# A transformer trunk on one core: the products with mod_w move from VectorE to TensorE, in strips of 32 columns, into the first mixer

## The chip, the cores and the metric

The kernel runs on one core of a Trainium2 chip. A core has TensorE (PE: matrix products into the eight banks of PSUM), VectorE (DVE), ScalarE (ACT), GpSimd (POOL) and SyncE (SP, which here issues the DMAs). Each works through a queue of its own in order, and semaphores tie them together. The metric is the device time of one execution in microseconds.

## What is computed

Two post-norm layers on a sequence of 512 tokens of width 1024. Before each of the four sub-layers (mixer and feed-forward in each layer) the input is scaled and shifted, and behind it the output is multiplied by a gate; all three come from a vector c:

```python
c_act = jax.nn.silu(c)
for l in range(DEPTH):
    mod = (c_act @ mod_w[l] + mod_b[l])[:, None, :]          # mod_w: (2, 1024, 6144)
    sh_m, sc_m, g_m, sh_f, sc_f, g_f = jnp.split(mod, 6, axis=-1)
    h = x * (1 + sc_m) + sh_m
    y = even_mixer(h, ...) if l % 2 == 0 else odd_mixer(h, ...)
    x = layer_norm(DEEPNORM_ALPHA * x + (1 + g_m) * y, ln_mix_g[l], ln_mix_b[l])
    h = x * (1 + sc_f) + sh_f
    y = conv_ffn(h, ...)
    x = layer_norm(DEEPNORM_ALPHA * x + (1 + g_f) * y, ln_ffn_g[l], ln_ffn_b[l])
```

The first mixer joins eight heads of sparse attention (an indexer keeps the best keys of a query by rounds of top-8) with eight heads of latent attention. The second is stick-breaking attention. mod_w is 48 MB in fp32 and is read once.

## The kernel before

All large products are made from float32r parts: an operand is split into a high and a low part, and a product is three (`mm3`: high-high, high-low, low-high). Weights come from DRAM by 128 x 512 tiles `raw`, are split by a cast to the high part on ACT (or DVE) and a subtraction on DVE or POOL into `whl`, and PE multiplies. Tensors stand transposed, 128 features by 512 tokens a tile. A product of two plain fp32 operands (the ones with `ones` or `ident`) needs more passes over the array; the trace shows it as two instructions, or as one where it is a transpose.

The stages in order of time: first projections (8 tiles of features, 7 banks open at once, from line 669; until about 73 us), late projections, index scores and top-k (until 168), four pairs of latent heads and four of sparse heads (until 300), the output product and norm (until 380), the feed-forward of layer 0 (up-projection until 612, down-projection and norm until 760), stick-breaking attention (until 1010) and its output and norm, then the feed-forward of layer 1.

**The products with mod_w.** In `m0` stand the shift and scale columns of the first mixer, which nothing can start without. For every k (128 features) ACT scales two of the eight 128 x 256 row blocks by columns of `ca` = silu(c), POOL adds them, DVE runs six more through `scalar_tensor_tensor` into half of the tile `xres` (named acc at line 672), and PE sums its 128 rows by products with a column of ones into the bank `cs`. From that come A_col and B_col, the scaled input hk, and its parts in `h`.

The other parts of mod_w go through `mod_acc` (line 937): for 512 columns at a time eight tiles `mraw` (two buffers) are loaded, and DVE adds m * ca to the tile `acc` (one buffer), eight `scalar_tensor_tensor` of 128 x 512. For parts 2 and 4 of layer 0, `shared`, the scaling and the sum are separate operations that POOL may take (`nc.lazy`). `mod_cols(dst)` sums the rows of four 128-column pieces by products with ones into columns and makes A_col and B_col of sub-layer dst; `mod_gate(i)` spreads the sum over all partitions with a 128 x 128 tile of ones and adds 1, into the tile `gate`. They run where the code calls them: gate 0 and columns 1 during the first mixer (with a bias MOD_BIAS of 1560 places in the order), gate 1 and columns 2 as filler of the first feed-forward, columns 3 and gate 2 between the heads of stick-breaking attention, gate 3 in the second feed-forward.

**What sets the order.** The class `Plan` records all engine calls and then issues them by a list schedule: at every step the engine whose clock is earliest takes the operation with the smallest place in the recorded order (plus `nc.bias`) among those whose inputs are there. It uses a price for every operation (`price`, line 200), a delay between engines (HOP), a model of DMA (360 bytes per ns, start, end), of PE's clock (`pe_time`), and of the SBUF ports that DVE and POOL share (`port`, `port_free`: an operation that would have to wait for the ports for longer than `tol` is passed over). Operations of `nc.either` and `nc.lazy` go to the engine that would end them first. So the emitted queues are fixed, and they are in the order that these prices give. Tiles of a tag take its buffers in recorded order (BUFS).

```python
            lhs, rhs = kw["lhsT"], kw["rhs"]
            op.work = size(rhs) * (1.6667 if lhs.dtype == F32 else 0.4167)
            if lhs.dtype == BF16:
                return max(op.work + 2.5, 56.0)
            return max(op.work + 2.5, size(lhs) * (1.6667 if lhs.dtype == F32 else 0.835))
```

Of the kernel before, what the change touches and what calls it, by code (L numbers as in the profile page):

```python
# [28 lines left out]
ROUNDS = min(256, S // 4) // 8  # L29
ALPHA = 4.0 ** 0.25  # L30
# [24 lines left out]
# ns from the end of an instruction to the start of one that waits for it  # L55
# [14 lines left out]
# what each hold of the SBUF ports shared by VectorE and GpSimd waits for  # L70
# [8 lines left out]
class Plan:  # L79
    """Records engine calls in program order and issues them in the order of a list schedule.  # L80

    Dependences are those of the recorded order (by tile and region); a tag's tiles take
    their buffers in the recorded order, so the schedule cannot run out of buffers where
    the recorded order does not.
    """
# [26 lines left out]
    # -- recording --  # L112
# [86 lines left out]
    # -- costs --  # L199
    def price(self, op):  # L200
# [42 lines left out]
    def port(self, op, e=None):  # L243
        """how an op holds the pair of SBUF ports that VectorE and GpSimd share"""
# [15 lines left out]
    # -- scheduling --  # L260
    def schedule(self):
# [21 lines left out]
        def offer(i):  # L283
            """op i has all its inputs; it can run once its new tiles have buffers"""
# [32 lines left out]
        def port_free(i, e):  # L317
            """when the pair of SBUF ports that VectorE and GpSimd share is free for op i"""
# [15 lines left out]
        def worth(i, e):  # L334
            """whether engine e would finish op i before any other that may run it"""
# [20 lines left out]
        def pe_time(op):  # L356
            """the time of a TensorE instruction at the clock that its activity allows"""
# [12 lines left out]
        while done < len(ops):  # L370
# [41 lines left out]
            op.start = clock[e]  # L412
            k = self.port(op)
# [35 lines left out]
class _Either:  # L449
    """Operations that several engines may run, whichever comes to it first."""  # L450
# [14 lines left out]
    def scale(self, out, src, by):  # L465
        """out = src * by, a column"""
# [3 lines left out]
    def norm(self, x, mean, scale, bias):  # L470
        """x = (x - mean) * scale in place; bias = -mean * scale"""
# [17 lines left out]
class Parts:  # L489
    """tiles of equal width that are indexed as one of shape [P, 2, columns]"""  # L490
# [21 lines left out]
def tile_trunk(ctx: ExitStack, tc: tile.TileContext, t: dict):  # L512
# [7 lines left out]
        "raw": 4, "whl": 6, "t2": 8, "hl": 9, "row": 2, "gate": 1, "mraw": 2, "acc": 1,  # L520
# [42 lines left out]
    def split(out_hi, out_lo, src, eng=nc.either):  # L563
        """src (on SBUF) = out_hi + out_lo"""
# [3 lines left out]
    def split_ps(out_hi, out_lo, src):  # L568
        """the same with src on PSUM"""
# [3 lines left out]
    def split_heads(tiles, src):  # L573
        """rows 64 h of src (on PSUM) into rows 0 of tile h"""
# [7 lines left out]
    def load_w(src, cols, eng=nc.lazy, tag="whl"):  # L582
        """a weight tile's float32r parts; src(lo, hi) gives its columns lo..hi on DRAM"""
# [22 lines left out]
    ones = const("ones", [P, P])  # L606
    nc.vector.memset(ones[:], 1.0)
    scr = tl("t2", [P, S])
    nc.gpsimd.memset(scr[:, 0:P], -1.0)
    nc.gpsimd.memset(scr[:, P:2 * P], -1.0)  # L610
    nc.gpsimd.affine_select(scr[:, P:2 * P], scr[:, P:2 * P], [[-1, P]], ALU.is_ge, 0.0, base=0, channel_multiplier=1)
    # negated ones and lower triangle, then the parts of the sparse values
    negs = const("negs", [P, 15, 64], F32R)
# [389 lines left out]
    def chain(*gens):  # L1003
        for g in gens:
            yield from g
# [628 lines left out]
```

## Time and profile before

| | us |
|---|---|
| median of 3 runs (lowest, highest) | 1409.38 (1405.83, 1412.77) |
| span of the profiled execution | 1414.6 |
| PE, DVE, ACT, POOL busy in it | 1337.3, 1102.1, 727.8, 333.9 |

The profile is of one execution; its span is 5.2 us above the median of the runs. A matmul's busy time reaches to the modelled end of its pipeline, so neighbours overlap, and the pace of products is read from one start to the next. All operations are recorded through one helper, so every instruction has line L446, and it is known by its tiles: `sc`, `tr`, `mm` and `md` are banks of PSUM, `t` are tiles t2, and buffer numbers are left out.

### The profile page before, as it was taken

Reading aid. Unit: us, or ns where it says so; the run is one execution under the profiler, and the core shown is the slowest. Engines: PE = TensorE matmul, PEld = TensorE weight load, DVE = VectorE, ACT = ScalarE, POOL = GpSimd, SP = SyncE. Lnnn points to the kernel's source line nnn. Section 1 sums busy time; section 2 is a strip of 40 time slices with the busy share of each in tenths; the row PEclk is TensorE's granted clock in tenths of the full one; section 3 lists DMA queues with packets and bytes.
Section 4 is the critical chain, followed back from the end, with each engine's and each line's share of the span. In section 5 each row is a group of like instructions: output and inputs, shape, how many; then the busy total and the mean of one; then the engine's idle time right before and its main releaser. Section 6 shows DMA issues by size and latency. Waiting matters only on the chain.

```text
span 1414.6 us, 21212 instructions
## 1 busy us (share of the span) xinstructions
PE 1337.3 (95%) x7468; PEld 1131.9 (80%) x7468; DVE 1102.1 (78%) x2030; ACT 727.8 (51%) x1376; POOL 333.9 (24%) x311
## 2 busy tenths in 40 slices
PE   4888799999899999999999999999969999999997
PEld 3666577887788999888877888878858999998885
DVE  6997997789898888883485886777688889994347
ACT  4355566753544444443334886788344555564230
POOL 4575866623611111020040100100041000020000
PEclk9987888999999999999999999999989999999999
DMA  9422433254155444553412243321305323242331
GB/s 323 149 66 65 131 97 107 90 165 134 60 165 170 133 156 153 174 168 107 134 42 93 75 146 112 108 82 60 104 30 176 116 98 120 89 150 93 101 105 59
DMA packets 88458, 166.54 MB, mean 118 GB/s; under 512 B 11128, under 2 KB 13688, under 8 KB 88352
## 3 DMA queue, kind: packets, MB, share of 16 engines
q1 hardware_dynamic: 88064, 165.14, 37.2%
q8 instruction: 58, 0.95, 0.3%
q14 instruction: 48, 0.39, 0.1%
q10 hardware_dynamic: 288, 0.06, 0.0%
HBM read 158.80 MB, written 2.10 MB: 114 GB/s over the span
## 4 chain that ended last, share of the span: by engine, by line
PE 71%; DVE 14%; issue 4%; ACT 4%; DMA 4%; POOL 2%; SPq 0%; DVEq 0%; POOLq 0%; ACTq 0%
PE sc L446 38%; PE tr L446 16%; PE mm L446 13%; PE md L446 4%; DVE t L446 4%; DVE xres L446 2%; DVE row L446 2%; ACT t L446 2%; DMA raw<-in_wup_dram 1%; DVE h L446 1%; DVE acc L446 1%; ACT qk L446 1%; DMA mraw<-in_mod_w_dram 1%; DVE hl L446 1%; DVE st L446 1%
## 5 line engine op out<-in xcount | busy, mean ns | idle before, releaser
L446 PE MATMUL sc<-h,whl 128*128 128x512 f32 (+1 forms) x2076 | 422.8, 359 | 7.8 <-ACT h L446 4.7
L446 PEld LDWEIGHTS sc<-h,whl 128*128 128x128 f32 x2076 | 348.7, 194 | 63.5 <-ACT h L446 5.5
L446 ACT CAST whl<-raw 128x512 fp32r<-128x512 f32 (+1 forms) x352 | 213.4, 613 | 264.0 <-PE sc L446 154.6
L446 DVE TENSOR_TENSOR whl<-raw,whl 128x512 fp32r<-128x512 f32 x296 | 207.8, 709 | 109.4 <-ACT whl L446 107.9
L446 POOL TENSOR_TENSOR whl<-raw,whl 128x512 fp32r<-128x512 f32 (+1 forms) x77 | 105.5, 1379 | 476.3 <-ACT whl L446 325.9
L446 DVE SCALAR_TENSOR_TENSOR acc<-mraw,ca,acc 128x512 f32<-128x512 f32 x118 | 98.0, 831 | 14.0 <-DMA mraw<-in_mod_w_dram 13.1
L446 POOL TENSOR_TENSOR rs<-rs,nhalf 128x1 f32<-128x1 f32 (+1 forms) x19 | 14.3, 754 | 328.5 <-DVE rs L446 328.4
L446 PE MATMUL sc<-whl,t 128*128 128x512 f32 x252 | 67.4, 393 | 0.3 <-ACT t L446 0.3
L446 ACT ACTIVATE t<-t 128x512 f32<-128x512 f32 x84 | 52.7, 637 | 19.5 <-DVE t L446 19.1
L446 DVE TENSOR_TENSOR raw<-raw,raw 128x512 f32<-128x512 f32 x86 | 59.1, 688 | 4.3 <-DMA raw<-in_wup_dram 2.8
L446 PE MATMUL mm<-h,whl 128*128 128x512 f32 x204 | 60.2, 435 | 1.2 <-ACT y L446 1.2
L446 ACT ACTIVATE t<-t,rs 128x512 f32<-128x512 f32 x16 | 13.0, 815 | 90.9 <-DVE rs L446 90.8
L446 PEld LDWEIGHTS sc<-whl,t 128*128 128x128 f32 x252 | 47.1, 188 | 11.3 <-DVE t L446 0.7
L446 PEld LDWEIGHTS mm<-h,whl 128*128 128x128 f32 x204 | 42.1, 212 | 11.5 <-ACT y L446 1.7
L446 ACT CAST hl<-t 128x512 fp32r<-128x512 f32 (+1 forms) x74 | 44.7, 627 | 5.4 <-DVE t L446 4.9
L446 PE MATMUL mm<-hl,V 128*128 128x128 f32 (+5 forms) x342 | 45.7, 276 | 1.2 <-ACT hl L446 0.9
L446 PEld LDWEIGHTS mm<-hl,V 128*128 128x128 f32 (+1 forms) x342 | 39.0, 168 | 8.0 <-ACT hl L446 2.1
L446 PE MATMUL tr<-whl,t 128*128 128x512 f32 x168 | 43.2, 391 | 0.0
L446 PE MATMUL mm<-whl,t 128*128 128x512 f32 x168 | 43.0, 391 | 0.0
L446 DVE SCALAR_TENSOR_TENSOR xres<-y,ca,xres 128x256 f32<-128x256 f32 x48 | 36.6, 773 | 8.0 <-POOL xres L446 7.2
L446 PE MATMUL tr<-h,whl 128*128 128x256 f32 (+1 forms) x240 | 40.1, 315 | 2.5 <-POOL whl L446 1.6
L446 PE MATMUL sc<-y,h 96*128 96x128 f32 (+3 forms) x96 | 34.4, 470 | 7.6 <-ACT y L446 3.2
(388 smaller groups left out, 2976.6 us busy)
## 6 DMA issues: line engine op xcount, KB each, us to landing
raw<-in_wup_dram SPq DMA_DIRECT2D x176, 256.0 KB, 3.4
mraw<-in_mod_w_dram SPq DMA_DIRECT2D x160, 256.0 KB, 2.9
raw<-in_wdown_dram SPq DMA_DIRECT2D x88, 256.0 KB, 2.9
y<-in_m_dram SPq DMA_DIRECT2D x16, 512.0 KB, 7.2
raw<-in_w_out_dram SPq DMA_DIRECT2D x32, 256.0 KB, 2.6
raw<-in_wqk_dram SPq DMA_DIRECT2D x32, 256.0 KB, 3.0
row<-in_ln_dram SPq DMA_DIRECT2D x8, 512.0 KB, 4.0
raw<-in_wqkv_dram SPq DMA_DIRECT2D x16, 256.0 KB, 3.0
```

Source lines behind the costliest of these rows:

```text
L446: getattr(getattr(self.nc, op.eng), op.fn)(*op.args, **op.kw)
```

## The change

The products with mod_w are made by PE with silu(c) as the stationary operand: a block of `cab` of 128 rows and 32 columns, one of which holds the values and the others zeros (a second row of the strip can be reached by shifting the window by one column, so that the two layers' gates share a strip). The result fills 32 partitions of a bank. Four column ranges of mod_w go to the four strips of partitions 0, 32, 64 and 96 of one bank. For `m0` the rows r and r + 4 share a strip, so the products of a k are eight of 32 x 256; ACT copies the bank to SBUF and the sum over the 128 rows by ones stays.

For the rest, `mod_rows` loads 128 x 512 tiles `mraw` (now four buffers) and makes one product of 32 x 512 with each: 32 for every `mod_cols`, 64 for the four gates together. Columns are then reached by four transposes of the bank's copy, gate rows wait in the constant tile `gate_rows` and are spread by a product of 32 rows (`sel`) when their gate is due. All of it is recorded behind the first projections with a bias of 200 places; only the spreading of a gate stays at its old place. `mod_acc` is gone, and with it the tags `acc` and `gate`; the bank `md` no longer serves the late projection and the norms of the latent vectors, which go to `mm` and `tr`. The constants `negones` and `negtri` are made later.

The planner changes in three places: a product with 32 stationary columns is priced at a quarter of its time, float32r products at some ns more, and DVE and POOL start an operation in the plan only once the ports are free. All else that the diff holds is removed comments.

```diff
@@ price
             lhs, rhs = kw["lhsT"], kw["rhs"]
             op.work = size(rhs) * (1.6667 if lhs.dtype == F32 else 0.4167)
+            if size(lhs) == COLS:
+                op.work /= P // COLS
+                return op.work + 2.5
             if lhs.dtype == BF16:
                 return max(op.work + 2.5, 56.0)
-            return max(op.work + 2.5, size(lhs) * (1.6667 if lhs.dtype == F32 else 0.835))
+            if lhs.dtype == F32:
+                return max(op.work + 2.5, size(lhs) * 1.6667)
+            return max(op.work + (13.0 if size(lhs) > 64 else 7.0), size(lhs) * 0.859)
@@ schedule
             op.start = clock[e]
+            if e in ("vector", "gpsimd"):
+                op.start = clock[e] = max(clock[e], port_free(i, e))
@@ tile_trunk
-        "raw": 4, "whl": 6, "t2": 8, "hl": 9, "row": 2, "gate": 1, "mraw": 2, "acc": 1,
+        "raw": 4, "whl": 6, "t2": 8, "hl": 9, "row": 2, "mraw": 4,
...
-    ca = const("ca", [P, KD])
-    nc.scalar.activation(ca[:], cT[:], AF.Silu)
+    cab = const("cab", [P, KD, COLS + 1])
+    nc.vector.memset(cab[:], 0.0)
+    nc.scalar.activation(cab[:, :, 1], cT[:], AF.Silu)
+    ca = lambda r, row: cab[:, r, 1 - row:1 - row + COLS]
...
         nc.bias = -150.0
-        acc = xa[:, 1, :].rearrange("p (a b) -> p a b", a=2)
-        row = lambda r: m0[r // 4][:, r % 4, :]
-        for r in range(MV_SPLIT, 8):
-            nc.scalar.mul(row(r), row(r), ca[:, r:r + 1])
-            if r > MV_SPLIT:
-                nc.gpsimd.tensor_tensor(acc[:, 1, :], row(r), acc[:, 1, :] if r > MV_SPLIT + 1 else row(MV_SPLIT), ALU.add)
-        nc.vector.scalar_tensor_tensor(acc[:, 0, :], row(0), ca[:, 0:1], acc[:, 1, :], ALU.mult, ALU.add)
-        for r in range(1, MV_SPLIT):
-            nc.vector.scalar_tensor_tensor(acc[:, 0, :], row(r), ca[:, r:r + 1], acc[:, 0, :], ALU.mult, ALU.add)
+        for r in range(KD):
+            g = r % 4
+            nc.tensor.matmul(cs[COLS * g:COLS * g + COLS, 0:256], lhsT=ca(r, 0), rhs=m0[r // 4][:, g, :], start=r < 4, stop=r >= 4, skip_group_check=True)
+        rk = xa[:, 1, 0:256]
+        nc.scalar.copy(rk, cs[:, 0:256])
...
+    def mod_rows(groups):
+        o = bank("md")
+        for i, (l, parts) in enumerate(groups):
+            for r in range(KD):
+                for g in range(4):
+                    lo = parts[g // 2] * D + (g % 2) * S
+                    m = tl("mraw", [P, S])
+                    nc.sync.dma_start(m[:], t["mod_w"][l, r * P:(r + 1) * P, lo:lo + S])
+                    nc.tensor.matmul(o[COLS * g:COLS * g + COLS, :], lhsT=ca(r, i), rhs=m[:], start=i == r == 0, stop=i == len(groups) - 1 and r == KD - 1, skip_group_check=True)
+        return o
+    def mod_cols(dst):
...
+        got = mod_rows([(l, (3 * sub_i, 3 * sub_i + 1))])
+        rows = tl("mraw", [P, S])
+        nc.scalar.copy(rows[:], got[:])
+        o = bank("md")
+        for j in range(4):
+            nc.tensor.transpose(o[:, j * P:(j + 1) * P], rows[:, j * P:(j + 1) * P], ident[:])
...
+    def mod_gates():
...
+        nc.vector.tensor_tensor(gate_rows[:], mod_rows([(l, (2, 5)) for l in range(2)])[:], gate_rows[:], ALU.add)
+    def mod_gate(i):
...
+            nc.tensor.matmul(o[:], lhsT=sel[rr, i // 2:i // 2 + 1].broadcast_to((COLS, P)), rhs=gate_rows[rr, :], start=True, stop=True)
+            nc.scalar.activation(g[:], o[:], AF.Identity, bias=ones[:, 0:1])
+    MOD_BIAS = 200.0
+    nc.bias = MOD_BIAS
+    mod_cols(1)
+    mod_gates()
+    mod_cols(2)
+    mod_cols(3)
...
-    us = ffn_up(0, h, chain(mod_gate(1), mod_cols(2)))
+    us = ffn_up(0, h, mod_gate(1))
...
-    steps = chain(mod_cols(3), mod_gate(2))
+    steps = mod_gate(2)
```

Where the change moves instructions on PE: first the head of its queue, the first projections. Before (`md_99` is cs, summed by ones from `xres`; sc, tr are banks of the projections):

```order
L446 MATMUL md_99<-ones,xres_102 128x1 x2
L446 MATMUL sc_92<-h_91,whl_103 128x512
L446 MATMUL sc_93<-h_91,whl_103 128x512
L446 MATMUL sc_92<-h_91,whl_103 128x512 x2
L446 MATMUL sc_93<-h_91,whl_103 128x512 x2
L446 MATMUL tr_94<-h_91,whl_103 128x512
L446 MATMUL md_99<-ones,xres_110 128x1 x2
```

and now (`y` holds m0, `cab` the strip):

```order
L454 MATMUL md_100<-y_101,cab 32x256 x4
L454 MATMUL md_100<-y_102,cab 32x256 x4
L454 MATMUL md_100<-ones,xres_103 128x1 x2
L454 MATMUL md_100<-y_109,cab 32x256 x4
L454 MATMUL sc_93<-h_92,whl_104 128x512
L454 MATMUL md_100<-y_110,cab 32x256 x4
L454 MATMUL sc_93<-h_92,whl_104 128x512 x2
```

The m0 products of a k stand in two groups of four, between the products of the k before.

Then PE at the late projections (`mm` are their banks). Before, one projection is followed by the next and by index scores:

```order
L446 MATMUL mm_316<-h_91,whl_312 128x512 x12
L446 MATMUL mm_316<-h_91,whl_313 128x512 x12
L446 MATMUL md_317<-ones,y_318 128x1
L446 MATMUL mm_326<-h_91,whl_322 128x512 x6
L446 MATMUL sc_215<-qk_199,hl_168 128x256
```

and now strips of the next sub-layer's columns (`md_166`) stand in between:

```order
L454 MATMUL md_166<-mraw_185,cab 32x512
L454 MATMUL mm_489<-h_92,whl_485 128x512 x3
L454 MATMUL md_166<-mraw_186,cab 32x512
L454 MATMUL mm_489<-h_92,whl_485 128x512 x5
L454 MATMUL md_166<-mraw_187,cab 32x512
L454 MATMUL mm_489<-h_92,whl_485 128x512 x2
L454 MATMUL md_166<-mraw_188,cab 32x512
L454 MATMUL mm_489<-h_92,whl_485 128x512 x2
L454 MATMUL mm_489<-h_92,whl_486 128x512
L454 MATMUL md_166<-mraw_189,cab 32x512
```

Such rows go on until the third pair of latent heads begins; of the 160 strips 132 have no other strip next to them.

Last, SP's queue behind the first weights of the late projections (`raw`); `t` to `t` are shuffles of 32 rows for the index scores. Before:

```order
L446 DMA raw_314<-in_winb_dram 128x512
L446 DMA raw_315<-in_winb_dram 128x512
L446 DMA raw_324<-in_winb_dram 128x512
L446 DMA raw_325<-in_winb_dram 128x512
L446 DMA t_89_172<-t_81_164 32x512 x2
L446 DMA t_89_172<-t_83_166 32x512 x2
```

and now:

```order
L454 DMA raw_502<-in_winb_dram 128x512
L454 DMA mraw_175<-in_mod_w_dram 128x512
L454 DMA raw_503<-in_winb_dram 128x512
L454 DMA mraw_176<-in_mod_w_dram 128x512
L454 DMA mraw_177<-in_mod_w_dram 128x512
L454 DMA mraw_178<-in_mod_w_dram 128x512
L454 DMA mraw_179<-in_mod_w_dram 128x512
L454 DMA t_265_350<-t_257_342 32x512 x2
```

Loads of mod_w now stand ahead of the shuffles and between the weights.

## Rows read from the trace of the kernel before

**Rows 1.** The page: busy time of each engine, and the granted clock by slices.

```profile
PE 1337.3 (95%) x7468; PEld 1131.9 (80%) x7468; DVE 1102.1 (78%) x2030; ACT 727.8 (51%) x1376; POOL 333.9 (24%) x311
...
PEclk9987888999999999999999999999989999999999
```

**Rows 2.** Stretches: window, its length, busy us (instructions) by engine, clock, DMA.

```profile
core 0: us, PE busy (x) PEld busy (x) DVE busy (x) ACT busy (x) POOL busy (x), PEclk, DMA share, GB/s
0.00:73.00 73.00, 51.52 (x209) 39.84 (x210) 58.40 (x104) 27.97 (x54) 36.86 (x40) 1.00 0.67 229
73.00:168.00 95.00, 80.64 (x310) 59.09 (x308) 82.71 (x154) 51.14 (x97) 70.88 (x57) 0.82 0.29 81
168.00:218.00 50.00, 44.68 (x267) 34.71 (x267) 46.28 (x126) 34.52 (x81) 32.80 (x38) 0.86 0.44 119
218.00:300.00 82.00, 79.53 (x572) 65.17 (x572) 63.30 (x215) 54.29 (x158) 46.70 (x64) 0.92 0.30 90
...
380.00:612.00 232.00, 230.22 (x1466) 209.22 (x1465) 200.28 (x327) 113.95 (x195) 34.14 (x28) 1.00 0.50 158
...
1010.00:1058.00 48.00, 36.95 (x199) 30.44 (x199) 40.41 (x80) 18.36 (x34) 17.64 (x14) 0.91 0.07 23
...
300.00:1414.60 1114.60, 1080.89 (x6116) 933.09 (x6115) 851.39 (x1435) 559.87 (x990) 146.68 (x116) 0.98 0.37 116
```

**Rows 3.** The chain of waits in 0 to 80 us: shares, and its first piece.

```profile
by line: DVE xres L446 26.8%; issue 16.8%; DVE row L446 14.8%; DMA y<-in_m_dram 7.3%; DMA raw<-in_wina_dram 6.7%; DVE t L446 5.7%; PE tr L446 3.5%; PE sc L446 3.3%; DVE whl L446 3.2%; PE mm L446 3.0%; PE md L446 3.0%; DVE h L446 1.9%; SPq L
...
1.72 5.86 DMA y<-in_m_dram
```

**Rows 4.** Groups of instructions: engine, operation, tiles, count, busy us, mean ns.

```profile
L446 DVE SCALAR_TENSOR_TENSOR acc<-mraw,ca,acc 128x512 f32<-128x512 f32 x118 | 98.0, 831 | 14.0 <-DMA mraw<-in_mod_w_dram 13.1 <-DVE whl L446 0.3
L446 DVE SCALAR_TENSOR_TENSOR xres<-y,ca,xres 128x256 f32<-128x256 f32 x48 | 36.6, 773 | 8.0 <-POOL xres L446 7.2
...
L446 POOL TENSOR_TENSOR acc<-acc,mraw 128x512 f32<-128x512 f32 x30 | 38.4, 1279 | 3.4 <-DMA acc<-in_mod_b_dram 1.8
...
L446 PE MATMUL md<-ones,acc 128*128 128x1 f32 x64 | 8.8, 247 | 0.4 <-DVE acc L446 0.4
...
L446 PE MATMUL mm<-ones,acc 128*128 128x1 f32 x32 | 3.8, 239 | 0.0
```

**Rows 5.** PE in order of time, a gate's fp32 product: start, us, tiles, rows*columns.

```profile
940.90 1.07 PE L446 MATMUL mm<-acc,ones 128*128 128x512 f32 x2
941.40 0.62 PE L446 MATMUL tr<-t,negs 128*128 128x128 f32 x1
941.87 0.39 PE L446 MATMUL tr<-hl,negs 128*128 128x384 f32 x1
```

**Rows 6.** PE in order of time: six fp32 transposes, 32 and 128 columns wide.

```profile
97.59 0.81 PE L446 MATMUL tr<-ident,t 128*32 128x128 f32 x6
...
188.33 0.84 PE L446 MATMUL tr<-ident,t 128*128 128x128 f32 x6
```

**Rows 7.** PE in order of time: products 64 columns wide among full ones.

```profile
826.63 0.39 PE L446 MATMUL sc<-qk,qk 128*128 128x512 f32 x1
826.86 0.98 PE L446 MATMUL mm<-hl,V 128*64 128x512 f32 x4
...
800.73 1.72 PE L446 MATMUL mm<-hl,V 128*64 128x512 f32 x11
802.29 0.44 PE L446 MATMUL mm<-qk,qk 128*128 128x512 f32 x1
```

**Rows 8.** PE in order of time: two products of 64 rows each.

```profile
803.09 0.50 PE L446 MATMUL mm<-row,qk 64*128 64x512 f32 x1
803.10 0.49 PE L446 MATMUL sc<-row,qk 64*128 64x512 f32 x1
803.52 0.96 PE L446 MATMUL sc<-h,whl 128*128 128x512 f32 x3
```

**Rows 9.** The chain of waits at 878 us: start, length, what.

```profile
878.41 10.88 PE sc L446 x48
```

**Rows 10.** DMA issues: count, size of each, median us to landing.

```profile
mraw<-in_mod_w_dram SPq DMA_DIRECT2D x160, 256.0 KB, 2.9
```

More of the change, by code (lines that the diff above doesn't have):

```diff
@@ L29 @@
 ROUNDS = min(256, S // 4) // 8
+COLS = 32
 ALPHA = 4.0 ** 0.25
@@ L703, in rope @@
+    MOD_BIAS = 200.0
[4 more added lines that the diff above has]
+    mod_cols(3)
+    nc.bias = 0.0
     def rope(x1, x2, parts, evac=True):
@@ L902, in rms @@
             rb = rbs[:, tt * P:(tt + 1) * P]
-            nc.vector.tensor_scalar(rb, ones[:], rs[:, tt:tt + 1], scale, ALU.mult, ALU.mult)
+            nc.vector.tensor_scalar(rb, ones[:].broadcast_to((P, P)), rs[:, tt:tt + 1], scale, ALU.mult, ALU.mult)
             nc.tensor.matmul(bc[:, tt * P:(tt + 1) * P], lhsT=rb, rhs=ident[:], start=True, stop=True)
-        out = tl("mraw", [P, S])
+        out = tl("hl", [P, S])
         nc.scalar.copy(out[:], bc[:])
@@ L933, in tile_trunk @@
     nc.bias = 0.0
-    mod_bank = ["md"]
-    def mod_acc(l, part, half, init):
-        shared = l == 0 and part in (2, 4)
-        acc = tl("acc", [P, S])
-        cols = slice(part * D + half * S, part * D + (half + 1) * S)
-        if init:
-            nc.gpsimd.memset(acc[:], 0.0)
-            nc.sync.dma_start(acc[0:1, :], t["mod_b"][l:l + 1, cols])
-        for r in range(KD):
-            m = tl("mraw", [P, S])
-            nc.sync.dma_start(m[:], t["mod_w"][l, r * P:(r + 1) * P, cols])
-            if shared:
-                if r == 0 and not init:
-                    nc.lazy.scale(acc[:], m[:], ca[:, 0:1])
-                else:
-                    nc.lazy.scale(m[:], m[:], ca[:, r:r + 1])
-                    nc.lazy.tensor_tensor(acc[:], acc[:], m[:], ALU.add)
-            elif r == 0 and not init:
-                nc.vector.tensor_scalar(acc[:], m[:], ca[:, 0:1], None, ALU.mult)
-            else:
-                nc.vector.scalar_tensor_tensor(acc[:], m[:], ca[:, r:r + 1], acc[:], ALU.mult, ALU.add)
-        return acc
@@ L984, in tile_trunk @@
-    gates = {}
-    def mod_gate(i):
-        l, sub_i = i // 2, i % 2
-        g = tl("gate", [P, D])
-        gates[i] = g
-        for half in range(2):
-            acc = mod_acc(l, 3 * sub_i + 2, half, True)
-            yield
-            o = bank(mod_bank[0])
-            nc.tensor.matmul(o[:], lhsT=ones[:], rhs=acc[:], start=True, stop=True)
-            nc.scalar.activation(g[:, half * S:(half + 1) * S], o[:], AF.Identity, bias=ones[:, 0:1])
-            yield
     def drain(gens):
@@ L1001, in drain @@
                 pass
-    def chain(*gens):
-        for g in gens:
-            yield from g
     nc.tol = 0.0
-    nc.bias = MOD_BIAS
-    drain([mod_gate(0), mod_cols(1)])
-    nc.bias = 0.0
     yT = [None] * 8
@@ L1112, in tile_trunk @@
         0: [tuple(va[:, i, j, :] for i in range(2)) for j in range(NT)],
[L1113 removed]
+        1: [tuple(negs[:, 4 * i + j:2 + 4 * i + j, :].rearrange("p a b -> p (a b)") for i in range(2)) for j in range(NT)],
     }
```

101 lines of the change are left out of this document (55 added, 46 removed).

## The prediction

> **What bounds the kernel now.** I read the page first. TensorE (PE) is busy 95% of the span, VectorE (DVE) 78%, and the granted clock stands at full speed except in the first quarter [rows 1]. The table of stretches says where PE has time left [rows 2]. From 300 us to the end it is busy 1080.9 of 1114.6 us, and in the up-projection of the first feed-forward (380 to 612) 230.2 of 232: there PE's own products set the time, and DVE's 200 us lie beside them. The one hole is the turn between the layers (1010 to 1058). The first mixer is different. In 73 to 218 us PE is busy 125 of 145 us, and at a mean granted clock of 0.82 and 0.86, which is part 1.2 and part 2.4 GHz; DVE and GpSimd (POOL) are nearly full. Before 73 us the chain of waits runs through DVE's sums into xres, which take 27% of the first 80 us [rows 3].
>
> So the place where the change can gain is the first mixer, and what it may not do is to give PE there more than the time it has left.
>
> **What is removed.** DVE loses 48 products into xres (36.6 us) and 118 into acc (98.0 us); POOL loses 30 sums into acc (38.4 us) and the scalings before them [rows 4]. Of the products into acc, most of DVE's stand after 380 us, beside a full PE; they are cover work there, not the path. PE loses the column sums, 64 + 32 instructions of 0.14 and 0.12 us [rows 4], 12.6 us in all, about 10 of them after 300 us. That is real gain, since PE is the bound there.
>
> **What is added, and its price.** PE gets 160 products of 32 x 512 in full fp32 and 64 of 32 x 256. The order shows where: all 160 stand between the end of the first projections and the start of the third pair of latent heads, which is 73 to 218 us of the kernel before. What one costs is the heart of the case. The kernel before has the same product 128 wide: two instructions, from 940.90 us to the next full-speed product but one at 941.87, with one 128-column transpose (0.11 us) between, so 0.86 us [rows 5]. Is a narrow one cheaper? Six fp32 transposes 32 wide take 0.81 us and six 128 wide 0.84 us [rows 6]: the time follows the columns that stream through, not the width of the result. So a strip costs 0.86 us by itself. The planner prices it at a quarter, 0.216 us, which is true only when four strips run side by side.
>
> Can they? Nothing in this trace shows two column strips at once. The nearest rows are row strips: two products with 64 rows each start 0.01 us apart, and the next one comes 0.42 us after the second [rows 8]. So neighbours in the queue do overlap. The Trainium skill agrees ("TensorE: Matmul & The Clock Gate", Part 3) with 2.38 times for three column strips of 512 columns. By the factor of 4 that it gives for a left operand of up to 32 columns ("TensorEngine Tiling (Array Packing)", Theoretical Speedup), the 160 products would be 34 us, an estimate from that page.
>
> But strips can only share the array with neighbours. A full-width product uses all columns, and by rows 7 a product after a narrow one starts only when that has streamed: eleven 64-wide products with 3328 columns in all hold the next one back by 1.56 us, against 1.39 us of pure streaming at 2.4 GHz. In the new order 132 of the 160 strips stand alone between full-width products; the rest are six pairs and runs of three, four and nine. Counting a pair, three or four as one turn and nine as three, that is 132 + 6 + 1 + 1 + 3 = 143 turns, 143 x 0.86 = 123 us. With no overlap at all it is 160 x 0.86 = 138 us.
>
> **The sum, against the profiled 1414.6 us.**
>
> Start, to 73 us. PE's work there is 51.5 us [rows 2]. The 64 small products stand in 16 groups of four, one after another in the queue, and a group's data are one load, so its four are ready together: 16 x 0.43 = 7 us if they overlap, 64 x 0.43 = 27.5 if not. The first rows land at 7.6 us [rows 3], so PE, no longer held by DVE, needs 8 + 51.5 + 7 = 66.5: -6 us. Without overlap it is +14. If the data come early and half of PE's present busy time was waiting, -13.
>
> The long stretch, 73 to 218. PE's busy time at full clock would be 80.6 x 0.82 + 44.7 x 0.86 = 104.5 us, so 40.5 of the 145 us are free [rows 2]; as busy time includes the overlapping tails of products (48 full ones take 10.88 us, 0.227 each [rows 9], and a single one is shown 0.39 long [rows 7]), I take 45, and 51 as its upper end. Then 123 - 45 = +78 us. Bounds: 138 - 40 = +98, and 0 if the strips cost the planner's 160 x 0.216 = 35 us, which fits in the free time.
>
> 218 to 300. No strip is left here, but POOL's and DVE's work on acc is gone; DVE is busy 63 of 82 us and PE 79.5 at 0.92, so 73 us of work. I take -10 us, with 0 and -18 as bounds (PE's work with the tails taken off is about 64).
>
> From 300 us. -10 us for the column sums. PE's idle time there is 33.7 us in all, 11 of it in the turn at 1010 us, where no modulation work stands; I take -6 for the rest, between 0 and -33. The eight products that spread a gate over the partitions stay (same 512 columns; their 32 rows add 0.2 us at the switch by rows 8, under 2 us together). DVE's and ScalarE's additions (a copy of the rows for each norm, adding the bias, filling small constants) are some 15 instructions under 0.7 us beside a full PE: nothing.
>
> In sum -6 + 78 - 10 - 10 - 6 = +46 us, so 1460.6 on the scale of the profile. That execution is 5.2 us above the median of the runs, 1409.38, so I predict **1455 us**.
>
> Queues. The loads of mod_w move up in SP's queue, ahead of weight loads and of the small shuffles that feed the index scores. Each waits until PE has used the buffer four loads back, so a late strip now holds everything behind it on SP. A load lands 2.9 us after its issue [rows 10], and four buffers give one strip every 1 us or so, faster than PE takes them. Nothing that PE needs soon stands there, as the order stretches with PE; price 0 to 10 us, in the width of the range.
>
> **Rivals.**
>
> *A strip alone costs a quarter*, the planner's price. Its 160 x 0.216 = 35 us then vanish in 73 to 218, and DVE and POOL, relieved, may give 10 us there: -6 - 10 - 10 - 16 = -42, 1367 us. It would need that a full-width product runs beside a strip, or that the strip streams faster; rows 6 and 7 speak against both. This ends faster.
>
> *No overlap at all*: +20 at the start, +15 in the stretch, 1490 us. Rows 8 speak against it.
>
> *A drain at every switch.* Row strips pay 0.2 us on the way back to full rows: 0.42 us from the second of rows 8 to the next, for 512 columns that stream in 0.21. If column strips do so, 143 x 0.2 = 29 us more, 1484. The 64-wide products show none: into them 0.23 us, the pace of full ones, and out of them at most 0.17 us for eleven [rows 7]. The Trainium skill says it generally, "changing tiling mode drains the TensorE" ("TensorEngine Tiling (Array Packing)", Key Properties); the trace agrees for row strips and not for 64 columns, and no row has 32-column strips on different columns.
>
> *DVE's relief pays the strips back.* If PE's tails hide more free time (51 instead of 45 us), 218 to 300 falls to its 64 us, and all PE idle after 300 goes: -6 + 72 - 18 - 10 - 33 = +5, about 1414, within 0.5%. It needs that DVE causes all PE idle; the hole at 1010 us speaks against that, for no removed work stands in it.
>
> **Chances and range.** Strips alone at full price with neighbours overlapping, 1430 to 1480: 0.62. No overlap 0.08. Drain 0.09. A quarter's price 0.13. Relief pays back 0.08. A measurement of this kernel can tell about 0.5% (7 us) from no change. Slower by more than that: 0.62 + 0.08 + 0.09 and a little of the last, less the main case's low edge, 0.78; within: 0.08; faster: 0.14. The range leaves out the quarter's price and the far end of the drains: 1395 to 1498.
>
> **What would show it.** In the profile after: the two fp32 instructions of a lone strip, start to the next product's start, 0.85 us or more (a quarter's price: 0.22); PE busy without holes at clock 1.0 from about 66 us until the third latent pair, which starts near 290 us instead of 218; the first projections done by 64 to 68 us; four strips of m0 in about 0.43 us at full clock; and after the mixer all stretches as long as before, less some 10 us. I am wrong at the root if the lone strips show 0.2 us, and wrong in size if PE is found waiting in that stretch (then SP's queue), or if the part after the mixer gets shorter by over 20 us.

## The result, and the profile after

The changed kernel takes **1531.07 us** (median of 4 runs, 1526.40 to 1536.58) against 1411.08 for the kernel before on the same chip: ratio 1.0851, 95% interval 1.0808 to 1.0894, +120 us. The forecast was 1455, +46: the direction was right, the size was not, and the time lies outside the range.

The page of the changed kernel (as [rows 1] of before: busy time, share, instructions; then the granted clock by slices):

```profile
PE 1485.7 (97%) x7832; PEld 1127.1 (73%) x7832; DVE 986.7 (64%) x1897; ACT 718.6 (47%) x1355; POOL 219.7 (14%) x216
...
PEclk9999999998999999999999999999998999999999
```

PE is busy for 148 us more, DVE for 115 and POOL for 114 us less, and of the slices at 7 and 8 tenths in the first quarter one is left, the tenth, at 8. The table of stretches of the changed kernel (as [rows 2]; the first mixer up to the third latent pair in two pieces, then its other heads, then all the rest):

```profile
68.00:218.00 150.00, 145.67 (x447) 51.70 (x446) 67.11 (x152) 46.91 (x88) 65.56 (x54) 1.00 0.64 190
218.00:342.00 124.00, 124.00 (x460) 48.45 (x460) 61.66 (x157) 36.14 (x84) 16.43 (x24) 1.00 0.60 176
342.00:421.00 79.00, 78.33 (x542) 61.52 (x542) 52.16 (x191) 52.74 (x153) 16.15 (x33) 0.94 0.10 30
421.00:1534.90 1113.90, 1077.52 (x6060) 926.16 (x6058) 776.93 (x1330) 559.24 (x988) 93.26 (x77) 0.98 0.27 86
```

From 68 to 342 us PE has no holes to speak of (269.7 of 274 us busy) at full clock, as forecast, but the forecast had it end near 290; DVE is busy less than half of it. Three borders in PE's order of time (start, length, tiles, count) give the stages. In the changed kernel:

```profile
67.21 0.84 PE L454 MATMUL mm<-h,whl 128*128 128x512 f32 x3
67.98 1.06 PE L454 MATMUL md<-mraw,cab 128*32 128x512 f32 x8
...
341.63 0.33 PE L454 MATMUL sc<-y,h 96*128 96x128 f32 x1
...
420.67 1.16 PE L454 MATMUL sc<-whl,y 128*128 128x512 f32 x4
```

and before:

```profile
70.57 0.84 PE L446 MATMUL mm<-h,whl 128*128 128x512 f32 x3
...
217.68 1.18 PE L446 MATMUL sc<-y,h 96*128 96x128 f32 x4
...
300.48 1.64 PE L446 MATMUL sc<-whl,y 128*128 128x512 f32 x6
```

The first border is the 168th product of `h` with a weight tile, since the first projections have 168: it starts at 67.7 us (before 70.8; there seven products of the late projections stand ahead of it, and the last one of the first projections starts at 72.4). The third latent pair starts at 341.6 (217.7), the output product at 420.7 (300.5; three of its products stand up to 19 us earlier in the changed kernel). So against the profiled execution of before: start -3.1, first mixer up to the third pair +127.0, from there to the output product -3.7, everything behind it +0.1; in sum +120.3, the difference of the spans (1534.9 and 1414.6). One caution: in the five comparisons told of here before's median was 1404.9 to 1411.1, so its profiled execution is 4 to 10 us long, and that of the changed kernel, the longest of its four, some 5; a stage difference of a few us is no finding.

**What a strip costs.** PE's order of time in the changed kernel, full products with strips between:

```profile
83.65 1.05 PE L454 MATMUL md<-mraw,cab 128*32 128x512 f32 x4
84.63 0.97 PE L454 MATMUL mm<-h,whl 128*128 128x512 f32 x3
85.53 1.05 PE L454 MATMUL md<-mraw,cab 128*32 128x512 f32 x2
...
87.16 1.04 PE L454 MATMUL md<-mraw,cab 128*32 128x512 f32 x2
88.14 1.67 PE L454 MATMUL mm<-h,whl 128*128 128x512 f32 x6
89.74 1.04 PE L454 MATMUL md<-mraw,cab 128*32 128x512 f32 x2
90.72 0.97 PE L454 MATMUL mm<-h,whl 128*128 128x512 f32 x3
91.61 1.05 PE L454 MATMUL md<-mraw,cab 128*32 128x512 f32 x2
...
93.48 1.04 PE L454 MATMUL md<-mraw,cab 128*32 128x512 f32 x2
94.46 0.73 PE L454 MATMUL mm<-h,whl 128*128 128x512 f32 x2
95.12 1.05 PE L454 MATMUL md<-mraw,cab 128*32 128x512 f32 x2
```

Read from strip to strip: with two full products between 1.64 us (93.48 to 95.12), with three 1.87 (89.74 to 91.61), with six 2.58 (87.16 to 89.74). So a full product is 0.235 us, near the 0.227 of [rows 9], and a lone strip's turn is 1.64 - 0.47 = **1.17 us**, not 0.86. Two strips side by side (x4, at 83.65) take the same: 83.65 to 85.53 with three products is 1.88. Lone strips take the same in all four places of the bank (0.975 to 0.979 us from the strip's start to the next product). The pieces, from the single records: 0.10 us more than usual from a full product to the strip, 0.98 from the strip to the next product, and 0.10 more from that to the one after. The expectations below say 1.08 (without the last piece) or 1.19 (with it). 140 turns x 1.18 and the one run of nine, which waited for its loads (9.8 us), are 175 us; the forecast had 123.

### The profile page after: what moved, and what is told of

It reads as the page before. It is cut to its first block, busy times and chain, and to the rows that moved or that the text cites. A ratio compares the mean times of both kernels' runs of the same rounds, so it can differ in the third digit from the quotient of the medians.

```text
span 1534.9 us, 21555 instructions
## 1 busy us (share of the span) xinstructions
PE 1485.7 (97%) x7832; PEld 1127.1 (73%) x7832; DVE 986.7 (64%) x1897; ACT 718.6 (47%) x1355; POOL 219.7 (14%) x216
## 4 chain that ended last, share of the span: by engine, by line
PE 85%; DVE 6%; ACT 4%; DMA 3%; issue 2%; POOL 1%; SPq 0%; DVEq 0%; POOLq 0%; ACTq 0%
PE sc L454 38%; PE mm L454 17%; PE tr L454 16%; PE md L454 13%; DVE t L454 2%; ACT t L454 1%; DMA mraw<-in_mod_w_dram 1%; ACT qk L454 1%; DVE h L454 1%; ACT hl L454 1%; DMA raw<-in_wup_dram 1%; DMA raw<-in_w_out_dram 1%; DVE st L454 1%; DVE row L454 1%; DVE xres L454 0%
## 5 line engine op out<-in xcount | busy, mean ns | idle before, releaser
L454 PEld LDWEIGHTS sc<-h,whl 128*128 128x128 f32 x2076 | 345.0, 193 | 65.8 <-issue 12.9
L454 DVE TENSOR_TENSOR whl<-raw,whl 128x512 fp32r<-128x512 f32 x321 | 222.3, 702 | 142.7 <-ACT whl L454 139.7
L454 PE MATMUL md<-mraw,cab 128*32 128x512 f32 x320 | 156.5, 605 | 3.8 <-DMA mraw<-in_mod_w_dram 3.4
L454 POOL TENSOR_TENSOR whl<-raw,whl 128x512 fp32r<-128x512 f32 (+2 forms) x52 | 65.7, 1269 | 214.8 <-ACT whl L454 122.5
L454 PE MATMUL mm<-h,whl 128*128 128x512 f32 x228 | 71.8, 422 | 0.0
L454 DVE TENSOR_TENSOR raw<-raw,raw 128x512 f32<-128x512 f32 x92 | 64.0, 696 | 3.7 <-DMA raw<-in_wup_dram 1.5
L454 PEld LDWEIGHTS md<-mraw,cab 128*32 128x32 f32 x320 | 20.7, 108 | 47.6 <-issue 31.2
L454 DVE TENSOR_TENSOR hl<-t,hl 128x512 fp32r<-128x512 f32 (+2 forms) x47 | 33.0, 729 | 30.4 <-ACT hl L454 20.3
L454 ACT CAST hl<-tr 128x128 fp32r<-128x128 f32 (+3 forms) x64 | 26.1, 424 | 55.2 <-PE tr L454 54.9
L454 DVE TENSOR_TENSOR hl<-tr,hl 128x128 fp32r<-128x128 f32 (+3 forms) x64 | 30.3, 487 | 30.7 <-ACT hl L454 30.4
```

The source lines that it names most:

```text
L454: getattr(getattr(self.nc, op.eng), op.fn)(*op.args, **op.kw)
```

## The experiments

Wide and small_after keep the order of the changed kernel to the last instruction, and small_quads that of quads_old. All other kernels here are planned anew, so their order differs elsewhere too, and each difference of theirs holds some of that.

**Is it the switch of width? (wide)** The order stays; only the emitted product changes (the line is shortened):

```diff
-matmul(o[COLS * g:COLS * g + COLS, :], lhsT=ca(r, i), rhs=m[:], ...)
+matmul(o[:], lhsT=ident[:], rhs=m[:], ...)
```

> Every product with mod_w is emitted at the same place in the same order, but with 128 stationary columns (the identity) and all 128 partitions of the bank as its result, so the modulation that comes out is not the reference's. Theory (0.10 us into a strip and 0.12 us out of it are the price of changing the width): a product costs 0.86 us and no more, neighbours no longer overlap, 160 x 0.86 = 138 us instead of the 168 that the 141 turns cost now: -31 us, 1500 us; 1490 to 1510. Rival (a full fp32 product among float32r products costs 1.08 us whatever its width): 141 turns as now and the 19 neighbours no longer hidden, +16 us, 1547.

Measured 1498.2 us, -33 against the changed kernel, as the theory said. PE in order of time:

```profile
86.11 1.02 PE L457 MATMUL md<-mraw,ident 128*128 128x512 f32 x2
86.57 1.95 PE L457 MATMUL mm<-h,whl 128*128 128x512 f32 x6
88.36 1.02 PE L457 MATMUL md<-mraw,ident 128*128 128x512 f32 x2
88.81 1.25 PE L457 MATMUL mm<-h,whl 128*128 128x512 f32 x3
89.91 1.02 PE L457 MATMUL md<-mraw,ident 128*128 128x512 f32 x2
```

Six products between: 2.25 us, three: 1.55; a full product is again 0.233, and the fp32 product takes 0.85. The same with 32 columns takes 1.17. So the strip costs 0.32 us more than a product four times as wide, and pays it once for a turn, not for each strip. Where it goes can be read from the weight loads (PEld) in order of time: in the changed kernel at a strip and behind it, in wide at the product of 88.36, and in the kernel before at the 32-wide transposes of [rows 6], behind the row strips of [rows 8] and at the 64-wide products of [rows 7].

```profile
87.16 0.14 PEld L454 LDWEIGHTS md<-mraw,cab 128*32 128x32 f32 x2 [0.36 <-issue]
88.14 0.77 PEld L454 LDWEIGHTS mm<-h,whl 128*128 128x128 f32 x4 [0.84 <-issue]
...
88.13 0.42 PEld L457 LDWEIGHTS md<-mraw,ident 128*128 128x128 f32 x2
...
97.36 0.76 PEld L446 LDWEIGHTS tr<-ident,t 128*32 128x32 f32 x6
...
803.52 0.53 PEld L446 LDWEIGHTS sc<-h,whl 128*128 128x128 f32 x3 [0.24 <-issue]
...
826.63 1.01 PEld L446 LDWEIGHTS mm<-hl,V 128*64 128x64 f32 x5
```

In wide the load starts 0.23 us ahead of its product (88.13, 88.36). In the changed kernel the strip's load starts with the strip (87.16), and that of the next full product with that product (88.14): across a turn no load runs ahead. The width by itself is not it: the 32-wide transposes have their load 0.23 us ahead (97.36, 97.59) and cost no more than wide ones [rows 6], and so have the 64-wide products (826.63, 826.86). Behind the row strips it is as behind a column strip (803.52, 803.52). What costs is going from full products to products laid out as column strips, and back. This is the rival "a drain at every switch" of the prediction, with 0.32 us in place of 0.2; what the array does in that time no run here shows.

**Do turns count, or strips? (pairs, quads)** In `mod_rows` the strips of one row block are kept together: in the plan the first depends on all their loads, and the others take the first place on PE once it is issued (the lines are shortened):

```diff
+lead.deps.update(x.idx for _, x in loads)
+for q in prods[1:]:
+    q.prio = -1e6
+    q.deps.add(lead.idx)
```

> The same with two strips kept together: 77 turns instead of 141. Theory: 64 turns fewer x 1.08 = -69 us, 1462 us; 1450 to 1475. Rival (each strip costs about 1 us wherever it stands): no change, 1515 to 1545.

> Four strips of one row block of mod_w are kept together: the first waits for all four loads, and the other three follow it at once, so 160 strips stand in 40 turns instead of 141. In the trace of the changed kernel a lone strip moves the next product by 1.08 us (0.10 into the strip, 0.98 from its start to the next product), and pairs of neighbours move it by the same 1.08 us, as their first instructions start 7 ns apart. Theory (what counts is the number of turns): 101 turns fewer x 1.08 = -109 us, 1422 us; 1405 to 1435. Rival (each strip costs about 1 us wherever it stands, and the order or the loads make the loss): no change, 1515 to 1545.

Pairs: 1466.5 us, 64.5 less than the changed kernel, as expected. Quads: 1459.0, only 72 less where 109 were expected. The miss can be read from PE's order of time in the kernel with four together:

```profile
66.87 1.06 PE L454 MATMUL md<-mraw,cab 128*32 128x512 f32 x8
67.87 4.83 PE L454 MATMUL mm<-h,whl 128*128 128x512 f32 x20
72.63 2.27 PE L454 MATMUL md<-mraw,cab 128*32 128x512 f32 x8
74.83 0.44 PE L454 MATMUL sc<-ident,t 128*128 128x128 f32 x2
```

The first group takes 1.00 us to the next product, the second 2.20. Its four loads are issued between 68.0 and 70.4 us, a load lands 3.8 us after its issue (median), and the last strip starts at 73.85: the later strips were not loaded yet, and PE, in order, waits. Summed over the 40 groups (from the product before to the product behind, less that product's own time) they take 79 us, where 40 x 1.08 would be 43. That is 36 of the 37 us.

**Is it the planner's price? (price)**

```diff
-    op.work /= P // COLS
-    return op.work + 2.5
+    return op.work + 222.0
```

> Only the planner's price of a strip changes, from 0.216 us to what a lone one takes, 1.08 us. The order that it makes then has 12 long runs of strips (up to 44 in a row) instead of 141 turns. Theory: with four buffers a run gets its tiles one at a time: the one run of nine in the changed kernel took 9.6 us, 1.06 us a strip, with TensorE waiting for loads. So 160 x 1.06 = 170 us, about what the 141 turns cost (168): 1531 us, 1510 to 1550. Rival (the loss comes from the planner's wrong price, which puts everything else in the wrong place): 1480 us or less.

Measured 1575.3 us, 44 more than the changed kernel: neither. With the full price the loads seem faster to the planner than PE, so strips stand in 12 long runs, and on the chip these wait for their loads. The first line of PE's list of waits (us in all, times, longest):

```profile
PE md L453 <- DMA mraw<-in_mod_w_dram: 43.3, 64, 1.7
```

and one row of such a run in order of time, with the idle time ahead of it and its cause:

```profile
91.49 3.43 PE L453 MATMUL md<-mraw,cab 128*32 128x512 f32 x4 [0.53 <-DMA mraw<-in_mod_w_dram]
```

The runs sum to 181 us, 1.13 a strip, close to the 170 expected; the rest is probably that nothing else is done in such a run, so the free time of the mixer is no longer filled (between 80 and 240 us PE is busy 123 of 160). A right price for one instruction did not mend the plan, since what it prices depends on the neighbours.

**What stands behind the turns? (out, noload, noload_old, small_after, small_quads, queue_act)** First, most strips are left out:

```diff
+if r in (0, KD - 1):
     nc.tensor.matmul(...)
```

> Of the eight row blocks of mod_w only the first and the last are multiplied (all tiles are still loaded), so the modulation is incomplete: 40 strips are left, in 28 turns. Start to start over the neighbours, a turn in the changed kernel adds 1.19 us, so 28 turns are 33 us. Theory A (PE has about 45 us free in the first mixer, and strips are hidden up to that sum): the strips vanish in the mixer, 1395 to 1408 us. Theory B (something else in the change makes the first mixer longer, some 25 us, since the kernel with 40 turns, 48 us, still stands 51 us above the kernel before): 1430 to 1445 us.

1460.6 us: theory A falls, and B asked for too little. The 28 turns, 33 us by their price, take 56 us in the trace (summed as above), and the kernel is as slow as with the groups of four. In its chain of waits between 66 and 346 us the loads stand first:

```profile
by line: DMA mraw<-in_mod_w_dram 30.3%; PE sc L454 16.4%; PE mm L454 15.2%; PE md L454 12.4%; SPq L454 6.8%; PE tr L454 6.6%; DMA y<-V 2.2%; issue 1.8%; ACT y L454 1.6%; DMA xres<-in_x_dram 1.3%; DVE t L454 1.1%; ACT h L454 1.0%; DVE row L4
```

So the loads go too (the loop skips the row block), and then the plan goes back (the two other edits of the planner undone):

```diff
+if r not in (0, KD - 1):
+    continue
```

> As the kernel with two of eight row blocks multiplied, but the tiles of the other six are not loaded either: 40 strips, 40 loads, 34 turns of 1.19 us (40 us). In that kernel 30% of the chain of waits between 66 and 350 us were loads of mod_w and 7% SyncE's queue. Theory (behind TensorE the 160 loads in SP's queue are the next bound of the first mixer): 25 to 35 us less than the 1461 of that kernel, 1425 to 1436; what is left above 1408 is the new plan. Rival (the loads cost nothing, only the plan): 1455 to 1470.

> The same, with the planner's prices and port rule as before: 40 strips, 40 loads, 36 turns (43 us). Theory (loads and plan together are all that stands behind the turns, and 45 us of TensorE are free in the first mixer): 1398 to 1412 us. Rival (something else in the change makes the mixer longer): 1425 us or more.

1443.3 and 1425.4: each removal is worth 15 to 18 us (counted from the kernel before of the same comparison). The first lands between theory and rival, the second at the rival's edge: 20 us over the kernel before stay, and 40 strips in 36 turns (43 us), packed into 65 to 152 us, hide only in part. One part of the answer is the granted clock. In out, and in noload_old, from the end of the first projections to the output product (columns as in [rows 2]):

```profile
68.00:346.20 278.20, 243.41 (x1204) 161.45 (x1196) 182.86 (x496) 134.06 (x322) 103.69 (x115) 0.87 0.60 189
...
65.00:317.80 252.80, 236.24 (x1205) 158.37 (x1204) 193.66 (x507) 129.12 (x311) 100.77 (x112) 0.91 0.28 84
```

Where PE has no holes, in the changed kernel, the clock is 1.00 up to the third pair. Here PE has 35 and 17 us of holes, and the clock is 0.87 and 0.91; in before it is 0.87 from 70.8 to 300.5 us. Now, of the 45 us that the prediction counts as free, 21 are not idle time but the low clock of before: its 125.3 us of busy PE are counted there as 104.5. These come only if the clock rises to full, and with few strips it hardly does. So the 43 us of strips meet some 20 to 30 us rather than 45; that this is what is left over is argued from the rows, not shown by a run of its own.

Then the bytes: every load brings an eighth, in the same place of the same order (both diffs shortened).

```diff
-dma_start(m[:], mod_w[..., lo:lo + S]);       matmul(..., rhs=m[:])
+dma_start(m[:, 0:64], mod_w[..., lo:lo + 64]); matmul(..., rhs=m[:, 0:64] eight times over)
```

Last, all bytes again, but from another queue, for which the plan books 100 ns an issue in place of 475:

```diff
-nc.sync.dma_start(m[:], t["mod_w"][...])
+nc.scalar.dma_start(m[:], t["mod_w"][...])
```

> The changed kernel, every instruction in its place, but each load of mod_w brings 64 of the 512 columns (an eighth of the bytes), and the product reads these 64 columns eight times over, so the modulation is not the reference's. Theory (the first mixer is bound by TensorE there, its turns cost 1.19 us whatever the loads do): 1531 us, 1522 to 1536; the run of nine strips, which waited for loads, may give back up to 7. Rival (loads share in the loss): 1510 or less.

> The same with four strips kept together, prices and port rule as before: the order of the kernel that took 1445 us, with an eighth of the bytes of mod_w. Theory (behind TensorE the transfer of the tiles is the next bound: with two of eight row blocks the loads' removal gave 17 us): 1422 to 1432. Rival (it is their place in SP's queue, with its waits for free buffers): 1438 to 1448.

> Four strips kept together, prices and port rule as before, all bytes, but the loads of mod_w are issued by ScalarE instead of SyncE. Theory (transfer is the bound): 1440 to 1452, no gain from another queue. Rival (it is their place in SP's queue): 1422 to 1434.

small_after: 1524.8, as the theory said: in the changed kernel the bytes are worth at most 6 us (the intervals of the two ratios, 1.0815 to 1.0855 and 1.0808 to 1.0894, overlap). small_quads: 1432.5 against 1445.1 for the same order with all bytes (quads_old, below), -13, at the edge of the theory; the groups sum to 54 us instead of 71. So the transfer of the tiles is a bound there. It accounts for 13 of the 38 us over the kernel before, and that the entries in SP's queue have a part in the other 25 is not excluded. queue_act: 1463.8, 19 us worse than from SP, outside both theories. Its chain of waits between 65 and 345 us has 5.2% in ScalarE's queue (quads_old: 1.2% in SP's); what ACT has to do may stand behind its loads. Why it is as much as 19 us stays open, and so it does not decide between the two.

**What is the new plan worth? (planner, quads_old, oldplan)** In the kernel before, the two planner edits alone (quads_old and oldplan undo the same lines in the kernel with four together and in the changed kernel):

```diff
+            if e in ("vector", "gpsimd"):
+                op.start = clock[e] = max(clock[e], port_free(i, e))
...
+            return max(op.work + (13.0 if size(lhs) > 64 else 7.0), size(lhs) * 0.859)
```

> The kernel before with the changes of the planner alone: float32r products at the new price, and DVE and POOL start an operation in the plan only once the ports are free. Theory A: worth nothing, 1401 to 1415 us. Theory B (it is the new plan that makes the first mixer longer): 1420 to 1435 us.

> The kernel with four strips kept together, but with the prices and the port rule of the planner as before (a strip still at a quarter). Theory A (the plan is not the cause): 1459 us, 1451 to 1466. Theory B (the new plan costs the mixer some 25 us): 1430 to 1440.

> The changed kernel with the planner's float32r prices and port rule as before (a strip still at a quarter): 151 turns instead of 141. The first mixer is bound by TensorE there, so a better plan for VectorE and GpSimd can't show in it: +10 turns x 1.19 = +12 us; after the mixer the old plan gave 4.5 us between two kernels with four strips kept together. Theory: +7 us, 1538, 1525 to 1545. Rival (the plan costs 24 us here as it does in the kernel before): 1505 to 1515.

planner: 1433.4 us, ratio 1.0173 (1.0140 to 1.0206): the plan alone costs the kernel before some 24 us. quads_old: 1445.1 against 1459.0, between the two theories: the plan costs 14 there. oldplan: 1533.4, 2 us more than the changed kernel (8, counted from the kernel before of each comparison), so the rival falls and the theory's +7 may hold. The rest of the kernel shows why. The rows (columns as in [rows 2]) start at the first `sc<-h,whl` of 128x256, behind which PE has the same number of instructions left in before, start and planner (5784), and in the changed kernel, small_after, oldplan and noload_old (5720); this is their order:

```profile
363.90:1414.60 1050.70, 1020.25 (x5786) 884.01 (x5784) 794.20 (x1331) 531.48 (x936) 123.16 (x98) 0.98 0.36 113
364.90:1408.30 1043.40, 1016.04 (x5785) 881.21 (x5784) 788.02 (x1329) 530.33 (x934) 118.47 (x94) 0.99 0.37 114
374.20:1431.90 1057.70, 1019.76 (x5786) 883.28 (x5784) 789.05 (x1326) 534.36 (x938) 119.54 (x95) 0.99 0.36 113
...
488.10:1534.90 1046.80, 1016.39 (x5722) 875.51 (x5720) 723.37 (x1234) 530.08 (x933) 68.74 (x59) 0.98 0.27 86
481.50:1523.30 1041.80, 1011.61 (x5722) 872.00 (x5720) 724.41 (x1237) 530.12 (x933) 71.04 (x59) 0.99 0.27 86
494.50:1533.00 1038.50, 1011.02 (x5721) 871.59 (x5720) 731.26 (x1244) 523.15 (x924) 77.70 (x63) 0.99 0.26 86
382.50:1420.60 1038.10, 1010.55 (x5722) 871.75 (x5720) 729.04 (x1244) 523.60 (x925) 78.28 (x62) 0.99 0.26 87
```

The changed kernel and small_after have one and the same order there and differ by 5 us, at clocks of 0.98 and 0.99; before and start, nearly the same on PE, differ by 7. So only this much is safe: without the modulation and with the old plan the stretch takes 1038 us, 5 to 12 less than before; with the new plan it takes 1042 to 1047, so the plan takes back 3 to 9; alone, in planner, the new plan costs it 7 to 14, and the first mixer some 10 (374.2 against 363.9 and 364.9). In oldplan ten more turns (151) stand in the mixer, and the border comes 6 us later.

**What is the start worth? (start)** In the kernel before, m0's sums on DVE are replaced by the changed kernel's eight products.

```diff
-nc.vector.scalar_tensor_tensor(acc[:, 0, :], row(r), ca[:, r:r + 1], acc[:, 0, :], ALU.mult, ALU.add)
+nc.tensor.matmul(cs[32 * g:32 * g + 32, 0:256], lhsT=cab[:, r, :], rhs=m0[r // 4][:, g, :], ...)
```

> The kernel before with m0 alone moved to TensorE (eight products of 32 x 256 for each k, in groups of four; the zero-padded columns stand in the buffer of acc). In the changed kernel the first projections end 3.1 us earlier than before. Theory: that is all that m0 is worth, 1405 us, 1400 to 1408. Rival (DVE without its 36.6 us of sums into xres lets the work behind the first projections begin earlier too): 1388 to 1398.

1409.9 against 1407.5, ratio 1.0012 (0.9996 to 1.0028): nothing that can be measured, less than even the theory. A group of four strips of m0 in the changed kernel, at a granted clock of 1.00 (0 to 68 us):

```profile
41.27 0.40 PE L454 MATMUL tr<-h,whl 128*128 128x512 f32 x1
41.59 0.64 PE L454 MATMUL md<-y,cab 128*32 128x256 f32 x8
42.16 1.43 PE L454 MATMUL tr<-h,whl 128*128 128x512 f32 x5
```

0.57 us to the next product and 0.1 on either side, 0.77 instead of 0.43: 16 such groups would take 12 us, not 7.

**A version for both? (hybrid)** Strips for m0 and, in turns of four, for columns 1 and gate 0; `mod_acc` on DVE for the rest; the old plan.

```diff
     mod_cols(1)
-    mod_gates()
-    mod_cols(2)
-    mod_cols(3)
+    gate_first()
...
-    us = ffn_up(0, h, mod_gate(1))
+    us = ffn_up(0, h, chain(mod_gate(1), mod_cols_dve(2)))
```

> The strips where TensorE has time, VectorE where it has cover: m0, columns 1 and gate 0 by TensorE (the last two as 48 strips in 12 turns of four, 12 x 1.19 = 14 us, in the first mixer), all other parts by VectorE in their old places, the planner's prices and port rule as before. Theory: the 14 us fit into TensorE's free time in the mixer, and VectorE is rid of 40 us there: 1390 to 1404 us. Rival (VectorE was not what the mixer waits for, so nothing is gained, and strips cost some of their time): 1405 to 1420.

1415.1 against 1404.9, ratio 1.0072 (1.0057 to 1.0088): slower, by some 10 us. But not in the mixer: the border of the rows above comes at 354.8 us, against 363.9 in before and 364.9 in start, so with twelve turns and 40 us less for DVE the part up to there is 9 to 10 us shorter in the traces. The loss stands behind it, where the stretch takes 1057.3 us, 7 to 14 more than in those two; why stays open. No kernel here beats the one before.

## Why the prediction was wrong

- **The price of a strip** is the step that failed: "143 x 0.86 = 123 us". The number of turns was right (141 runs of strips; the 143 count the run of nine as three). The price left out the switch, 0.32 us, 45 us over all turns, which wide shows; the run of nine that waited for loads (9.8 us where three turns, 2.6, stood) is the other 7: 175 instead of 123. The prediction had weighed the switch from two rows: 64-wide products that showed none, and row strips that showed 0.2 [rows 7, 8]. It took the first as the nearer and gave the second 0.09, with 1484 us as its time, which was also too little. The nearer row was the second, and the weight loads of before could have told so: behind the row strips the load starts with its product, as behind a column strip, and at the 64-wide ones 0.23 us ahead (the last two rows of the loads under wide). The rule quoted there from the Trainium skill ("TensorEngine Tiling (Array Packing)", Key Properties) holds here with 0.32 us, there and back.
- **The free time** was right. Up to the third pair the stage took 274 us, 172 of it strips (three turns come later), so PE's own work is 102 of the 147 us it took before: 45 us free, as forecast. It was counted at full clock, and that holds only while PE is the bound throughout: in noload_old the strips are 43 us, no more than is free, and the output product still comes 17 us late (317.8 against 300.5), at a clock of 0.91.
- **That neighbours overlap, and alone they don't pay a quarter**: right. First instructions of neighbours start 7 ns apart, pairs cost what one does, and the rivals of a quarter's price and of no overlap are out. So is, for this kernel, the one in which DVE's relief pays the strips back; where the strips fit into PE's free time (hybrid), the part up to the feed-forward does get 9 to 10 us shorter.
- **The start** -6: -3 in the trace, no gain by itself. The groups cost some 12 us, not 7.
- **218 to 300**, -10: -3.7, with three turns (3.5 us) in it, so about -7.
- **After 300**, -16: nothing. A gain is there (5 to 12 us, noload_old and oldplan), but the new plan takes 3 to 9 of it back, and the prediction had given the planner's two other edits no term at all; alone they cost the kernel before 24 us. This is the second step that failed.
- **SP's queue**, 0 to 10: the loads' bytes are worth at most 6 us (small_after); the queue by itself was not measured in this kernel.

In sum, forecast and measured by the trace: start -6, -3; the mixer +78, +127; to the output product -10, -4; the rest -16, 0; together +46, +120. Of the difference of 74, 52 are strips, of which 45 are the switch, and 16 are the gain after 300 us that did not come, of which the plan explains 3 to 9.

## What to carry to other kernels

Count the times that the array goes over to strips and back, not the small products: here a lone strip between full ones cost its whole streaming time plus the switch, and four that stood together, with all their data there, cost hardly more than one. Another model of the machine inside a greedy scheduler is a change of its own: it reorders everything, and has to be timed alone. And free time on an engine can be spent only while that engine is the bound; after that the next one (here the loads, then the plan, with a lower clock in PE's holes) keeps what is left.

## What the runs showed of the hardware

- Strips of 32 columns on different columns run fully side by side: four products of 128 x 512 in fp32 start 7 ns apart and take 1.19 us together (1.00 from the first to the next full product, at 66.87 in the kernel with four together), one alone takes 1.17. The trace agrees with the factor of 4 of the Trainium skill ("TensorEngine Tiling (Array Packing)", Theoretical Speedup), but only without the switch: against four full-width products (4 x 0.85) it is 2.9.
- The switch between full products and column strips costs 0.32 us there and back, in three pieces of 0.10 to 0.12: before the strip, between the strip and the next product, and between that one and the next. Products 32 or 64 columns wide that are not laid out as strips showed none [rows 6, 7]. The last piece does not show in the strip's own rows. On either side of a strip the weight load starts with its product, not a product ahead (87.16 and 88.14).
- The start of a float32r product behind a full-width fp32 one seems to be recorded early (0.46 us after the fp32 product's first instruction, at 86.57 in the rows of wide), though the pair of instructions takes 0.85. Durations here are to be read over a whole cycle.
